# Running sums of a chunked down projection: kept in SBUF by VectorE, or in device memory by GpSimd's accumulating transfers

## The chip, the cores and the metric

The kernel runs on one core of a Trainium2 chip. The metric is the device time in microseconds (us). The kernel before takes 1972.66 us, the median of 3 runs (1972.44 to 1972.72). The engines are called PE (TensorE), ACT (ScalarE), DVE (VectorE), POOL (GpSimd) and SP (SyncE, which here issues transfers only).

## The reference: what is computed

One layer of a hybrid backbone on 128 context tokens and 256 latent tokens, with D_MODEL = 2048: an adaLN modulation, a mixing sub-layer (gated linear attention and a Fourier branch), and a feed-forward sub-layer. The change is in the second half of the last one:

```
h = rmsnorm(x, lw['norm_pre_ffn']) * (1.0 + sc2) + sh2
ff = (jax.nn.silu(h @ lw['w_ffn_gate']) * (h @ lw['w_ffn_up'])) @ lw['w_ffn_down']
x = x + ga2 * rmsnorm(ff, lw['norm_post_ffn'])
```

The hidden width is FFN_HIDDEN = 5632. All inputs and outputs are float32.

## The kernel before

All 384 tokens are worked on together, as three tiles of 128. The weights come from device memory once, in tiles of 128 x 1024 float32 (512 KB). Each tile is split into a rounded part `whi` (a cast by ACT, line 1393) and the rest `wlo` (a subtraction by DVE, line 1404), and each product is the sum of three matmul passes (whi with the high and the low part of the activations, wlo with the high part). `whi` and `wlo` have four buffers each, and the raw tiles have two (`raw`) or stand in eight resident places (`u...`). A tile of weights is therefore cast when the PE has finished the tile four steps earlier.

The hidden width is cut into NFC = 11 chunks of 512 columns. Chunk 0's hidden values are computed first, in another layout. Then the list `steps` is worked off, one weight tile per step. For each chunk c from 1 to 10 it holds steps A and B (four each), then C, E, D four times, then F, G, H, D four times. A, B, C, E, F, G and H compute the gate and up products of chunk c (seven products of half-size blocks instead of eight). Each D step multiplies the hidden values of chunk c - 1 by one tile of w_d: 18 matmuls of 128 x 512 (line 1492), and two D steps (kh = 0, 1) make one group n of 512 output columns in three PSUM tiles `pdn`, one for each token tile t. There are four groups n per chunk, so 12 tiles of 128 x 512. At the end stand eight D steps for chunk 10 alone, in the order n = 0, 2, 1, 3 (`d_order`).

The output sums lie in SBUF, in two tiles named `psums`; `unit(t, n)` is the place of one 128 x 512 tile. Products of chunks 0 to 9 are handled by `out` (lines 1566 to 1571), which frees the PSUM tiles. Small operations such as these are put in a list `pend`. `split_next` takes up to three of them between the cast and the subtraction of the next weight tile; whatever is left is taken before the next pair of D steps begins. Products of chunk 10 are added by `add_last` (line 1561), which also makes the sum of squares for the norm. Before chunk 10 begins (line 1578), `x1b`, the residual, is read from device memory in four transfers (line 1583). After the last product follow the norm factors, transposes on the PE (lines 1670 and 1672), the residual addition (DVE line 1706, or ACT line 1699 with POOL line 1700) and the output writes (line 1711).

Program order is kept on PE, ACT, DVE and POOL. The instructions of SP, which issues all loads, are put in order by a scheduler; each of them waits in a queue until its buffer is free. The loads of raw tiles are line 1363, those of the resident places line 1371, and those of the last modulation vector (`ada_last`, worked in between the steps) line 1430.

Of the kernel before, what the change touches and what calls it, by code (L numbers as in the profile page):

```python
# [11 lines left out]
F32 = mybir.dt.float32  # L12
# [3 lines left out]
ALU = mybir.AluOpType  # L16
# [4 lines left out]
P = 128  # L21
# [75 lines left out]
def tile_step(ctx: ExitStack, tc: tile.TileContext, a, o):  # L97
    nc = tc.nc
    PE, ACT, DVE, POOL, SP = nc.tensor, nc.scalar, nc.vector, nc.gpsimd, nc.sync
# [5 lines left out]
    dram = ctx.enter_context(tc.tile_pool(name="dram", bufs=1, space=DRAM))  # L105
# [138 lines left out]
    def step(side):  # L244
        if side is not None:
            next(side, None)
# [595 lines left out]
    with ExitStack() as s:  # L842
# [166 lines left out]
        for b, i in mix_order:  # L1009
# [9 lines left out]
            else:  # L1019
# [3 lines left out]
                p = psm.tile([P, T], F32, tag="mm", name="pmm")  # L1023
# [16 lines left out]
    with ExitStack() as s:  # L1040
# [94 lines left out]
        u = pd.tile([P, 2, 3], F32, name="u12", bufs=1)  # L1135
# [141 lines left out]
        def unit(t, n):  # L1277

            return psums[n // 2][:, 3 * (n % 2) + t, :]
# [10 lines left out]
        pend, now = [], []  # L1290

        def left_sums():

            raw = [psums[n // 3][:, 2 * (n % 3) : 2 * (n % 3) + 2, :].rearrange("p a (b c) -> p (a b) c", c=P) for n in range(4)]
            f = lambda x: x.bitcast(F32)
            h11, h12, h21, h22 = ([f(x) for x in Hx(t, k)] for t, k in ((1, 0), (1, 8), (2, 0), (2, 8)))
            r1, r2, r4, r3 = raw
            add, sub = DVE.tensor_add, DVE.tensor_sub

            def parts(dst, src):  # L1300
                return [lambda: ACT.copy(dst[0], src), lambda: sub(dst[1], src, f(dst[0]))]
# [22 lines left out]
        d_order = (0, 2, 1, 3)  # L1324
# [88 lines left out]
        def grab2(kept=2):  # L1413
            w = take()
            while now:
                now.pop(0)()
            load_more(kept)
            split_next()
            return w
# [52 lines left out]
        for u in range(HEAD):  # L1472
            kind, c, j = ffn_order[u]
            dst_of[kind](hp[u], c, j)
        n = 0
        for kind, c, j in ffn_order[HEAD:]:
            p = psm.tile([P, T], F32, tag="mm", name="pmm")
# [83 lines left out]
        def add_last(t, n, p, done):  # L1561

            DVE.tensor_add(unit(t, n), unit(t, n), p)
            ACT.activation(ep[0], unit(t, n), AF.Square, accum_out=ssq[:, t, done : done + 1])

        def out(u, p, c):
            if c == 0:
                ACT.copy(u, p)
            else:
                DVE.tensor_add(u, u, p)  # L1570
            d_live[0] -= 1

        rate[0] = 0.85
        ada = paced(ada_last(), rate)
        pd_tiles, hid_last, x1b, done = None, None, None, 0
        for kind, c, i in steps:
            last_c = c == NFC - 1 and kind == "D"
            if last_c and hid_last is not None and x1b is None:
                while pend:
                    pend.pop(0)()  # L1580
                x1b = actp.tile([P, KT, T], F32, tag="A_hi", name="x1b")
                for q in range(4):
                    SP.dma_start(x1b[:, 4 * q : 4 * q + 4, :], x1_d[:, 4 * q : 4 * q + 4, :])
                ACT.activation(tmp1, eps_t, AF.Sqrt)
            if kind == "D":
                w = grab2()
                n, kh = i // 2, i % 2
                if kh == 0:
                    while pend:
                        pend.pop(0)()  # L1590

                    pool, tag = (pss, "side") if done % 2 or (c, n) == (NFC - 2, 3) else (psm, "mm")
                    pd_tiles = [pool.tile([P, 512], F32, tag=tag, name="pdn") for _ in range(3)]
                    d_live[0] = 3
                h = hid_last if last_c else hid
                todo = [
                    (pd_tiles[t], [[x[:, 2 * kh + m, t * P : (t + 1) * P] for m in range(2)] for x in h], mov_d, kh == 0, kh == 1)
                    for t in range(3)
                ]
                products(w, todo, by_tile=last_c and kh == 1)  # L1600
                if kh == 1:
                    if not last_c:
                        for t in range(3):
                            pend.append(lambda u=unit(t, n), p=pd_tiles[t], c=c: out(u, p, c))
                    else:
                        if done < 3:
                            for t in range(3):
                                pend.append(lambda t=t, n=n, p=pd_tiles[t], d=done: add_last(t, n, p, d))
                        if done == 1:
                            pend.append(lambda: DVE.tensor_add(r3, ssq[:, :, 0], ssq[:, :, 1]))  # L1610
                        if done == 2:
                            pend.append(lambda: DVE.tensor_add(r3, r3, ssq[:, :, 2]))
                        done += 1
                if not last_c and i >= 4:
                    step(ada)
                if (c, i) == (NFC - 2, 6):

                    while pend:
                        pend.pop(0)()
                    hid_last = tuple(actp.tile([P, FC, T], F32R, tag=t, name="hidE") for t in ("C_hi", "C_lo"))  # L1620
                    for t in range(3):
                        turn_hid(hid_last, t, psm, "mm")
            else:
                if kind == "A" and i == 0:
                    banks(c)
                w = grab2()
                products(w, [(bank[c, n], two_of(stat, i), mov_gu, first and i == 0, i == 3 and last) for n, stat, first, last in of_kind[kind]])
                if i == 3:
                    evict(c, kind)
                if kind == "B" and c > 1 and i < 3:  # L1630

# [13 lines left out]
        n = d_order[-1]  # L1645
# [144 lines left out]
```

## Time and profile before

| What | Value |
|---|---|
| Median of 3 runs | 1972.66 us (1972.44 to 1972.72) |
| Profiled execution, first to last instruction | 1970.6 us |
| Median of the runs less that span | 2.1 us |
| Granted TensorE clock, mean | 0.999 |
| Bytes moved by transfers | 380.06 MB, mean 193 GB/s |
| Of these by SP's queue (q1) | 377.92 MB, 57.3% of 16 engines' span |
| GpSimd's own queue | not used |

The profile is of one execution. A row of a group gives the source line, the engine, the operation, output <- inputs, shapes and the number of instructions, then the busy time, the mean duration of one in ns, and the idle time of the engine just before them with what ended it. In a row of the order of time the first number is the start in us, the second the duration; an idle time before the instruction stands in brackets. Matmuls are pipelined: one of 128 x 512 is shown with 389 ns, and the next starts 227 ns after it (18 of them take 4.08 us).

### The profile page before, as it was taken

To read this page: it belongs to the slowest core of one execution; us is meant where nothing else is said; L and a number is where in the kernel's file an instruction comes from. 1 tells how busy PE (TensorE), PEld (TensorE's weight loads), DVE (VectorE), ACT (ScalarE), POOL (GpSimd) and SP (SyncE) were. 2 spreads that over 40 slices of the span, in tenths; PEclk is the share of its full clock that TensorE was granted. 3 is DMA by queue.
4 is the path that set the end of the run, shared out by engine and by line. 5 is a ranking of instruction groups with operands and counts; after the bars stand their busy time and mean duration, and the time that the engine had idled before them with its cause. 6 is when DMAs were issued, how large, how long until landed. Compare 5 with 4: busy or idle time off the path is not lost.

```text
span 1970.6 us, 27516 instructions
## 1 busy us (share of the span) xinstructions
PE 1949.7 (99%) x10576; PEld 1727.3 (88%) x10576; DVE 1629.0 (83%) x2075; ACT 908.9 (46%) x1281; POOL 32.2 (2%) x44
## 2 busy tenths in 40 slices
PE   8999999999999999999999999999999999999998
PEld 6779999999999999999988888888888888888886
DVE  5569788878767878877789998999899989887875
ACT  4233554544345655446454444354444444444444
POOL 0000000000000000004000000000000000000001
PEclk9999999999999999999999999999999999999999
DMA  9978677767755687555435444453536363626243
GB/s 389 369 258 271 219 254 238 234 217 247 232 182 180 195 296 233 203 171 180 142 133 183 145 148 156 160 182 123 190 131 201 104 204 109 205 75 192 74 160 130
DMA packets 189411, 380.06 MB, mean 193 GB/s; under 512 B 14172, under 2 KB 112668, under 8 KB 184928
## 3 DMA queue, kind: packets, MB, share of 16 engines
q1 hardware_dynamic: 189136, 377.92, 57.3%
q8 instruction: 83, 1.36, 0.3%
q14 instruction: 48, 0.39, 0.1%
q10 hardware_dynamic: 144, 0.39, 0.1%
HBM read 361.48 MB, written 16.78 MB: 192 GB/s over the span
## 4 chain that ended last, share of the span: by engine, by line
PE 93%; DVE 3%; ACT 2%; DMA 1%; issue 1%; SPq 0%; POOL 0%; DVEq 0%; ACTq 0%; POOLq 0%
PE pmm L252 33%; PE pgu L1492 30%; PE pdn L1492 18%; PE pv L392 3%; PE pgm L375 1%; DMA slab<-in_w_ada 1%; PE px L410 1%; PE pmm L1246 1%; PE ptr L1553 1%; PE pf L990 1%; DVE wlo L219 1%; ACT whi L218 1%; PE po L639 1%; DMA raw<-in_w_d 0%; PE pf L991 0%
## 5 line engine op out<-in xcount | busy, mean ns | idle before, releaser
L252 PE MATMUL pmm<-A_hi,whi 128*128 128x384 f32 x1200 | 404.2, 337 | 0.0
L252 PE MATMUL pmm<-A_hi,wlo 128*128 128x384 f32 x1200 | 401.3, 334 | 0.0
L252 PE MATMUL pmm<-A_lo,whi 128*128 128x384 f32 x1200 | 401.2, 334 | 0.0
L1393 ACT CAST whi<-u 128x1024 fp32r<-128x1024 f32 x200 | 210.6, 1053 | 286.8 <-DVE u L1377 86.2
L1393 ACT CAST whi<-raw 128x1024 fp32r<-128x1024 f32 x175 | 184.3, 1053 | 199.0 <-PE pgu L1492 60.4
L218 ACT CAST whi<-raw 128x1024 fp32r<-128x1024 f32 x181 | 189.9, 1051 | 176.6 <-DMA raw<-in_w_gate 62.4
L1404 DVE TENSOR_TENSOR wlo<-u,whi 128x1024 fp32r<-128x1024 f32 x200 | 243.8, 1219 | 33.0 <-ACT whi L1393 17.8
L219 DVE TENSOR_TENSOR wlo<-raw,whi 128x1024 fp32r<-128x1024 f32 x179 | 217.9, 1221 | 62.1 <-ACT whi L218 61.7
L1492 PE MATMUL pgu<-whi,A_hi 128*128 128x512 f32 x640 | 250.0, 391 | 0.0
L1492 PE MATMUL pgu<-whi,A_lo 128*128 128x512 f32 x640 | 249.3, 389 | 0.0
L1404 DVE TENSOR_TENSOR wlo<-raw,whi 128x1024 fp32r<-128x1024 f32 x175 | 213.2, 1218 | 34.8 <-ACT whi L1393 25.4
L252 PEld LDWEIGHTS pmm<-A_hi,whi 128*128 128x128 f32 x1200 | 225.3, 188 | 2.5 <-issue 1.4
L252 PEld LDWEIGHTS pmm<-A_lo,whi 128*128 128x128 f32 x1200 | 225.4, 188 | 0.2
L252 PEld LDWEIGHTS pmm<-A_hi,wlo 128*128 128x128 f32 x1200 | 225.3, 188 | 0.0
L566 DVE SCALAR_TENSOR_TENSOR adacc<-adaw,spad,adacc 128x1024 f32<-128x1024 f32 x180 | 222.7, 1279 | 0.6 <-DMA adaw<-in_w_ada 0.4
L1492 PE MATMUL pdn<-whi,hid_hi 128*128 128x512 f32 x480 | 186.9, 389 | 0.0
L1492 PE MATMUL pdn<-whi,hid_lo 128*128 128x512 f32 x480 | 186.8, 389 | 0.0
L1492 PE MATMUL pgu<-wlo,A_hi 128*128 128x512 f32 x640 | 184.2, 389 | 0.0
L1492 PEld LDWEIGHTS pgu<-whi,A_hi 128*128 128x128 f32 x640 | 120.1, 188 | 26.1 <-issue 0.8
L1492 PEld LDWEIGHTS pgu<-wlo,A_hi 128*128 128x128 f32 x640 | 120.1, 188 | 25.4
L1492 PEld LDWEIGHTS pgu<-whi,A_lo 128*128 128x128 f32 x640 | 120.2, 188 | 25.1
L1492 PE MATMUL pgu<-whi,S 128*128 128x512 f32 x480 | 131.1, 395 | 0.0
(367 smaller groups left out, 2768.2 us busy)
## 6 DMA issues: line engine op xcount, KB each, us to landing
adaw<-in_w_ada SPq DMA_DIRECT2D x96, 512.0 KB, 4.4
raw<-in_w_d SPq DMA_DIRECT2D x88, 512.0 KB, 3.7
slab<-in_w_ada SPq DMA_DIRECT2D x32, 1024.0 KB
raw<-in_w_gate SPq DMA_DIRECT2D x64, 512.0 KB, 4.6
raw<-in_w_g SPq DMA_DIRECT2D x48, 512.0 KB, 3.2
raw<-in_w_u SPq DMA_DIRECT2D x48, 512.0 KB, 3.4
raw<-in_w_in SPq DMA_DIRECT2D x44, 512.0 KB, 3.5
u<-in_w_u SPq DMA_DIRECT2D x40, 512.0 KB, 4.7
```

The source lines that it names most:

```text
L218: ACT.copy(hi, raw)
L219: sub = lambda: eng.tensor_sub(lo, raw, hi.bitcast(F32))
L252: PE.matmul(dst, w[wi][:, k * n + n0 : k * n + n0 + P], x[xi][:, k0 + k, :], start=first and k == 0 and j == 0, stop=last and k == kts - 1 ...
L375: PE.matmul(pgv[q : q + 32, :], spad[:, k, :], slab[k // (KT // 2)][:, k % (KT // 2), :], start=k < 4, stop=k >= KT - 4,)
L392: PE.matmul(pv[2 * t + g], hT[x_][:, kb, t * P : (t + 1) * P], w_[:, g * 512 : (g + 1) * 512], start=kb == 0 and j == 0, stop=kb == KT - 1 ...
L410: PE.matmul(px, w_[:, u * P : (u + 1) * P], hT[x_][:, kb, :], start=j == 0, stop=j == 2)
L566: DVE.scalar_tensor_tensor(acc[:, c, :], w, spad[:, k, c : c + 1], acc[:, c, :], op0=ALU.mult, op1=ALU.add,)
L639: PE.matmul(dst, w[wi], x[xi], start=first and j == 0, stop=last and j == 2)
L990: PE.matmul(pf[:, 0 : 2 * HT], w[0][:, c], x[k], start=k == 0, stop=False)
L1393: ACT.copy(hi, src)
L1404: DVE.tensor_sub(lo, src, hi.bitcast(F32))
L1492: PE.matmul(dst, stat[x_][m], mov(w[w_], m), start=first and w_ == m == x_ == 0, stop=last and w_ == m == 1,)
```

## The change

The function `out` no longer adds into SBUF. ACT copies each product tile, of chunk 0 and of all others, into a staging place; the six tiles of the groups n = 1 and n = 3 serve as two staging places of three tiles, used in turn. For chunk 0 SP writes the staged tile to a new tensor `sums_d` in device memory. For chunks 1 to 9 GpSimd issues a transfer that adds the staged tile to the tile in device memory. Before chunk 10 begins, SP reads all twelve sums back into `unit(t, n)`, in the order of `d_order`, and `add_last` goes on as before. Lines below 1563 are shifted by up to 13 in the changed kernel.

```
+        sums_d = dram.tile([3, 4, P, 512], F32, name="sums_d")
+        turn = [0]
+
+        def out(t, n, p, c):
+
+            u = unit(t, 1 + 2 * (turn[0] // 3 % 2))
+            turn[0] += 1
+            ACT.copy(u, p)
             if c == 0:
-                ACT.copy(u, p)
+                SP.dma_start(sums_d[t, n], u)
             else:
-                DVE.tensor_add(u, u, p)
+                POOL.dma_start(sums_d[t, n], u, accum_op=ALU.add)
             d_live[0] -= 1
+
+        def sums_back(n):
+            for t in range(3):
+                SP.dma_start(unit(t, n), sums_d[t, n])
...
                 while pend:
                     pend.pop(0)()
+                for n in d_order:
+                    sums_back(n)
                 x1b = actp.tile([P, KT, T], F32, tag="A_hi", name="x1b")
...
-                            pend.append(lambda u=unit(t, n), p=pd_tiles[t], c=c: out(u, p, c))
+                            pend.append(lambda t=t, n=n, p=pd_tiles[t], c=c: out(t, n, p, c))
```

The built order of the changed kernel has the same matmuls in the same order on the PE. DVE has 108 instructions fewer, ACT 108 more, POOL 108 transfers more (all between its last work of the layer before and the six additions of the tail), and SP 24 transfers more: 12 writes and 12 reads. The reads of n = 0 stand in SP's order after the fourth-last load of w_u, those of n = 2 and n = 1 among the loads of w_d that follow the last load of w_u, and those of n = 3 after the four loads of x1b and ahead of the last four loads of w_d.

More of the change, by code (lines that the diff above doesn't have):

```diff
@@ L1564, in add_last @@
             ACT.activation(ep[0], unit(t, n), AF.Square, accum_out=ssq[:, t, done : done + 1])
-        def out(u, p, c):
+        sums_d = dram.tile([3, 4, P, 512], F32, name="sums_d")
[4 more added lines that the diff above has]
+            ACT.copy(u, p)
             if c == 0:
-                ACT.copy(u, p)
+                SP.dma_start(sums_d[t, n], u)
             else:
-                DVE.tensor_add(u, u, p)
+                POOL.dma_start(sums_d[t, n], u, accum_op=ALU.add)
             d_live[0] -= 1
+        def sums_back(n):
+            for t in range(3):
+                SP.dma_start(unit(t, n), sums_d[t, n])
         rate[0] = 0.85
```

## Prediction

> **What bounds the kernel now.** I read the shares first, then the chain that ended last, then the busy time by stretch of the stage that is changed.
>
> ```profile
> span 1970.6 us, 27516 instructions
> ...
> PE 1949.7 (99%) x10576; PEld 1727.3 (88%) x10576; DVE 1629.0 (83%) x2075; ACT 908.9 (46%) x1281; POOL 32.2 (2%) x44
> ...
> PE 93%; DVE 3%; ACT 2%; DMA 1%; issue 1%; SPq 0%; POOL 0%; DVEq 0%; ACTq 0%; POOLq 0%
> ```
>
> TensorE is busy in 99% of the span and makes up 93% of the chain. VectorE, which the change relieves, is second with 83%. A share is an average, so the question is whether TensorE ever waits in the feed-forward stage. The busy time by stretch (columns: PE, PEld, DVE, ACT, POOL, granted clock, DMA share, GB/s) shows three chunks of that stage, the end of the last mixed chunk, the chunk of w_d alone and the tail:
>
> ```profile
> 995.90:1090.34 94.44, 94.44 (x424) 78.21 (x423) 83.74 (x88) 48.17 (x57) 0.00 (x0) 1.00 0.50 163
> ```
> ```profile
> 1090.34:1185.28 94.94, 94.94 (x439) 78.12 (x438) 85.89 (x95) 44.18 (x48) 0.00 (x0) 1.00 0.46 148
> 1185.28:1279.22 93.94, 93.94 (x422) 77.76 (x421) 85.66 (x97) 39.91 (x42) 0.00 (x0) 1.00 0.50 162
> ...
> 1845.86:1920.55 74.69, 74.69 (x338) 61.92 (x337) 59.50 (x63) 34.04 (x37) 0.00 (x0) 1.00 0.43 149
> 1920.55:1953.77 33.22, 33.09 (x145) 26.76 (x143) 17.02 (x25) 13.89 (x29) 0.00 (x0) 1.00 0.28 106
> 1953.77:1970.60 16.83, 8.25 (x65) 7.24 (x64) 9.92 (x31) 7.96 (x23) 5.87 (x6) 0.95 0.48 188
> ```
>
> In each stretch up to 1920.55 the PE column equals the length, at a clock of 1.00: TensorE does not wait at all while VectorE is at 91%. From 1920.55 to 1953.77 it lacks 0.13 us. A waiting weight load in that stage is listed once, with 0.6 us:
>
> ```profile
> PEld pdn L1492 <- DVE hidE L1555: 0.6, 1, 0.6
> ```
>
> So VectorE time that is taken out here has no stall behind it to shorten. A busy PE need not be a PE at its peak, but its pace here is set by its own matmuls.
>
> **The change part by part.** *Removed:* 108 VectorE adds.
>
> ```profile
> L1570 DVE TENSOR_TENSOR psums<-psums,pdn 128x512 f32<-128x512 f32 x108 | 67.6, 680 | 12.3 <-PE pdn L1492 12.3
> ```
>
> They are 67.6 us of busy VectorE, and by the stretches above worth 0 on the path.
>
> *Added on ScalarE:* 108 copies of the same tiles. The trace has the very operation, because the products of chunk 0 are copied today:
>
> ```profile
> L1568 ACT COPY psums<-pdn x12: 572/590/606, 1016.7 to 1070.5; 128x512 f32<-128x512 f32 x12
> ```
> ```profile
> 1015.70 1.05 ACT L1393 CAST whi<-raw 128x1024 fp32r<-128x1024 f32 x1 [3.32 <-DMA raw<-in_w_g]
> 1016.66 1.56 ACT L1568 COPY psums<-pdn 128x512 f32<-128x512 f32 x3
> ```
>
> Three take 1.56 us, so 36 groups are 36 x 1.56 = 56 us of ScalarE, spread over ten stretches in which it is busy about 45%. The first stretch above (995.90 to 1090.34) is the one with these twelve copies, at the same places in the step order, and TensorE is busy 94.44 of 94.44 us in it. So the copies, and the later casts queued behind them, cost 0. The spare that hides them can be read at one weight tile of w_g:
>
> ```profile
> 1851.77 0.37 SPq L1363 DMA_DIRECT2D raw<-in_w_g  x1
> ```
> ```profile
> 1855.51 1.06 ACT L1393 CAST whi<-raw 128x1024 fp32r<-128x1024 f32 x1 [2.12 <-PE pdn L1492]
> ```
> ```profile
> 1857.35 1.22 DVE L1404 TENSOR_TENSOR wlo<-raw,whi 128x1024 fp32r<-128x1024 f32 x1
> ```
> ```profile
> 1864.95 4.08 PE pgu L1492 x18
> ```
>
> The cast waits for the buffer of the tile four steps earlier (the w_d step before), so this tile belongs to the step that starts at 1864.95, and it is ready at 1857.35 + 1.22 = 1858.6. That is 6.4 us early. A delay under 6 us of a cast or a load is hidden here.
>
> *Added on the queues:* 12 plain writes by SyncE (chunk 0), 108 accumulating transfers by GpSimd, 12 reads by SyncE, 256 KB each. GpSimd's only row in the stage says that it sat idle for 1025.59 us before the tail,
>
> ```profile
> 1958.33 1.96 POOL L1700 TENSOR_TENSOR x1b<-x1b,ep 128x384 f32<-128x384 f32 x2 [1025.59 <-ACT ep L1699]
> ```
>
> so its instructions delay nothing but each other. The staging place is used again two groups later, about 2 x 94.4 / 4 = 47 us, so a copy would wait only for a transfer that takes longer than that. The trace has no accumulating transfer; the nearest rows are these (KB each, median us from issue to landing):
>
> ```profile
> w<-in_w_ada SPq DMA_DIRECT2D x64, 256.0 KB, 2.5
> gates_d<-gz SPq DMA_DIRECT2D x32, 192.0 KB, 3.8
> gate<-gates_d SPq DMA_DIRECT2D x32, 192.0 KB, 3.9
> ```
> ```profile
> raw<-in_w_d SPq DMA_DIRECT2D x88, 512.0 KB, 3.7
> ```
>
> Lower end: a plain 256 KB move, 2.5 us. Upper end: a read of the old value and a write one after the other, scaled to 256 KB, (3.8 + 3.9) x 4/3 = 10.3 us, and for the last of three behind each other two more moves of 2 x 256 KB at the 3.7 us of a 512 KB load of w_d (last row): 10.3 + 7.4 = 17.7. I take a load plus a write, 2.5 + 3.8 = 6.3 us, since the three of a group overlap and the load row is the one with the right size. The Trainium skill, "DMA: Bandwidth & Descriptors", section "Anatomy of one DMA — SWDGE (gpsimd) path", fits a GpSimd transfer with about 2.0 us plus bytes / 436e3; for 256 KB that makes an estimate of 2.6 us, by which the sum would be the same and its spare larger. No run so far shows such a transfer.
>
> Volume: 12 transfers of a chunk, each counted twice for the old value, are 12 x 0.262 x 2 = 6.3 MB. The second stretch moves 148 GB/s at a share of 0.46, so 322 GB/s when busy; 6.3 MB are 20 us, and the share goes from about 0.48 to 0.69. No queue saturates.
>
> *Moved: SyncE's queue at the end.* This is the tightest place. In the built order of the changed kernel the reads of n = 0 stand behind the load that is issued at 1869.39 today. Those of n = 2 and 1 stand between the loads of w_d issued at 1896.40 and 1913.69. Those of n = 3 stand behind all x1b loads and **ahead of the last four w_d loads**, which are issued from 1921.15 today:
>
> ```profile
> 1869.39 0.37 SPq L1363 DMA_DIRECT2D raw<-in_w_u  x1
> ```
> ```profile
> 1896.40 0.37 SPq L1363 DMA_DIRECT2D raw<-in_w_d  x1
> 1904.75 0.37 SPq L1363 DMA_DIRECT2D raw<-in_w_d  x1
> 1907.71 3.29 SPq L1363 DMA_DIRECT2D raw<-in_w_d  x2
> ```
> ```profile
> 1917.22 0.95 SPq L1583 DMA_DIRECT2D x1b<-x_d  x2
> 1921.15 11.37 SPq L1363 DMA_DIRECT2D raw<-in_w_d  x4
> ```
> ```profile
> 1899.44 1.88 DVE L1570 TENSOR_TENSOR psums<-psums,pdn 128x512 f32<-128x512 f32 x3 [1.27 <-PE pdn L1492]
> ```
>
> n = 2: the tiles are free at 1899.4, ScalarE has copied by about 1901.7, and at 6.3 us the last transfer lands at 1908.0. The load of 1904.75 waits only for the first one (1900.6 + 6.3 = 1906.9, 2.2 us late), the next pair for the last (0.3 us late). Both are under the 6 us of spare: 0.
>
> n = 3: its last product tile is done as the first hidE matmuls start, and today the cast behind the wait is this:
>
> ```profile
> 1920.55 3.31 PE L1492 MATMUL pdn<-whi,hidE 128*128 128x512 f32 x12
> ```
> ```profile
> 1918.65 1.55 ACT L1555 CAST hidE<-ptr 128x512 fp32r<-128x512 f32 x3
> ...
> 1921.63 1.03 ACT L1393 CAST whi<-raw 128x1024 fp32r<-128x1024 f32 x1
> 1926.90 1.05 ACT L1393 CAST whi<-raw 128x1024 fp32r<-128x1024 f32 x1 [4.24 <-DMA raw<-in_w_d]
> ```
>
> ScalarE goes on to the three copies at 1920.2 and ends them near 1922.0. The cast of 1921.63 slips about 2 us; its step comes at 1932.8, so 0. The last transfer lands at 1922.0 + 6.3 = 1928.3; three reads are issued in 3 x 0.35 = 1.05 us; the fifth w_d load goes out at 1929.4, 8.2 us later than today. With the 5.75 us that it takes today (1921.15 to 1926.90, beside the x1b traffic) it lands at 1935.1, and its cast ends at 1936.1. The steps are 18 matmuls or 4.08 us, so step five starts at 1920.6 + 4 x 4.08 = 1936.9. Spare 0.8 us: the stall is max(0, L - 7.1) for a transfer time L. At 6.3 it is 0, at 2.5 it is 0, at 17.7 it is 10.6 us. The loads behind it follow at the pace of two buffers and lose no more. The sums of n = 3 are wanted here, and are back near 1933; the tail is untouched:
>
> ```profile
> 1951.09 0.69 DVE L1563 TENSOR_TENSOR psums<-psums,pdn 128x512 f32<-128x512 f32 x1 [3.74 <-PE pdn L1492]
> ```
>
> **Sum.** Own time: span 1970.6, and 2.1 us around it to the median of 1972.66 (1972.44 to 1972.72). Removed 0, copies 0, traffic 0, n = 2 0, n = 3 0 to 10.6 with 0 taken. I add 0.6 us for a spare of only 0.8 us under new traffic (an estimate: the reads' 0.75 MB at 322 GB/s are 2.3 us, of which 2.3 - 0.8 = 1.5 would show if all fell on the load; I take less than half). Prediction **1973.3 us**.
>
> **The rivals.**
>
> *Slower 1: the last wait in SyncE's queue.* If a transfer needs 11 us or more after its copy, the four w_d loads come too late: at 12 us 4.9 us of stall, 1977.6; at 17.7 us 1983.3. It decides from 7.1 us, and is a measurable loss from 11. For it: nothing else lies between the reads and the loads. Against it: the rows of 2.5 to 3.9 us. 0.18.
>
> *Slower 2: weight loads slowed by the transfers in every chunk.* It needs more than the 6.4 us of spare. If three transfers held the engines 7.4 us, 36 x 1.0 = 36 us, 2009. Against it: the load of 1921.15 took 5.75 us beside x1b, about 2 us more than usual, and TensorE did not wait. The Trainium skill speaks for it, in "DMA: Bandwidth & Descriptors", section "Issuing engines are not separate DMA queues": transfers of all issuing engines run on the same 16 engines and interleave. 0.08.
>
> *Slower 3: the transfers don't keep up.* Three must be through in 94.4 / 4 = 23.6 us, 7.9 each. At 10 us each a group lacks 6.4 us, 36 groups 230 us, 2200. 0.03.
>
> *Faster.* A gain of over 0.2% needs 3.9 us of TensorE's waits in this stage, and 0.6 us are listed. It would have to come from matmuls that run faster beside a quieter VectorE:
>
> ```profile
> L1492 PE MATMUL pdn<-whi,hid_hi 128*128 128x512 f32 x480 | 186.9, 389 | 0.0
> ```
>
> The stage is ten stretches of some 430 matmuls (424, 439, 422 above); 1 ns less on each of 4300 is 4.3 us, 1968.4. Nothing in the trace points to it. 0.03.
>
> *The change does nothing:* the forecast, with chance 0.68; the VectorE time comes out idle.
>
> **How the numbers follow.** Within 0.2% (1968.7 to 1976.6, about what a measurement of this kernel can tell from no change): 0.68. Slower: 0.18 + 0.08 + 0.03 = 0.29. Faster 0.03. The range goes from 1971.8 (the median less the 0.6 us wait and a little) to 1983.5, the upper end of the unknown transfer time; what lies beyond is slower 2 and 3 and faster, 0.14.
>
> **What would show it.** Right: DVE about 68 us less, ACT about 56 us more, TensorE's column equal to the length in the stretches up to 1920, transfers under 7 us, and no wait of the PE on whi after 1936. Wrong: a wait of SyncE at the reads of n = 3 longer than 9 us with the casts of the fifth w_d tile after 1937; casts that wait for raw tiles all over the stage; copies that wait for a transfer out of their staging place; or, for the gain, matmuls shorter than 389 ns.

## The result, and the profile after

The changed kernel is slower: 1980.73 us, the median of 4 runs (1980.45 to 1982.1), against 1972.69 us (1972.44 to 1973.94, 4 runs) for the kernel before on the same chip. The ratio is 1.0042, 95% interval 1.0028 to 1.0057: 8.0 us. The profiled execution of the changed kernel has a span of 1979.1 us, 8.5 more than before.

The page of the changed kernel (shares, GpSimd's queue, shares of the chain):

```profile
PE 1950.5 (99%) x10576; PEld 1726.2 (87%) x10576; DVE 1569.2 (79%) x1967; ACT 955.5 (48%) x1389; POOL 127.6 (6%) x152
...
q0 software_dynamic: 15552, 28.32, 9.5%
...
PE 74%; issue 16%; DVE 3%; DMA 2%; POOL 2%; ACT 2%; SPq 0%; DVEq 0%; POOLq 0%; ACTq 0%
```

TensorE has the same work (1950.5 us against 1949.7) and VectorE 59.8 us less. No engine is busier in a way that makes 8.5 us; the loss must be idle time of TensorE. The busy time by stretch, with the stretches laid at the marks of the changed kernel, shows where it is (same columns as before):

```profile
995.90:1090.34 94.44, 94.44 (x424) 78.17 (x424) 83.73 (x88) 47.87 (x57) 0.00 (x0) 1.00 0.58 196
1090.34:1185.28 94.94, 94.94 (x440) 78.12 (x439) 79.49 (x83) 49.77 (x60) 10.74 (x12) 1.00 0.68 181
1185.28:1279.22 93.94, 93.94 (x422) 77.75 (x422) 78.58 (x84) 45.32 (x54) 10.58 (x12) 1.00 0.70 195
1845.71:1924.91 79.20, 76.19 (x341) 62.22 (x339) 54.49 (x54) 37.93 (x46) 7.93 (x9) 1.00 0.68 193
1924.91:1961.71 36.80, 33.48 (x145) 26.80 (x145) 16.80 (x28) 17.19 (x37) 2.65 (x3) 1.00 0.52 157
1961.71:1979.10 17.39, 8.25 (x64) 7.23 (x64) 8.52 (x26) 6.74 (x19) 5.87 (x6) 0.82 0.47 182
```

In the ordinary chunks the PE column is still the whole length, though the DMA share is 0.68 to 0.70. In the last mixed chunk TensorE lacks 79.20 - 76.19 = 3.01 us, and in the chunk of w_d alone 36.80 - 33.48 = 3.32. The last stretch is longer with the same 8.25 us of matmuls. Here are the same two stretches of the kernel before, between the same marks, and its tail; TensorE lacks nothing in the first and 1.75 us in the second, 1.62 of them at its end, where the norm factor is awaited in both kernels:

```profile
1845.26:1920.32 75.06, 75.06 (x341) 62.33 (x339) 59.87 (x63) 34.18 (x38) 0.00 (x0) 1.00 0.44 148
1920.32:1955.40 35.08, 33.33 (x147) 26.96 (x145) 18.66 (x31) 15.35 (x33) 0.00 (x0) 1.00 0.28 103
1955.40:1970.60 15.20, 8.24 (x64) 7.23 (x64) 8.51 (x26) 6.74 (x19) 5.87 (x6) 0.95 0.53 208
```

So the span's 8.5 us fall into pieces. The marks are five rows of each trace: the first product matmul of the stage (`pdn`), the transposes that end chunk 9's hidden values (line 1553), the first and the last row of the hidE weight loads, and ScalarE's issue of the last output write. Between the last hidE weight loads and that issue every profile has 12.98 to 13.01 us, so this piece is left out. The table has all profiled runs; the labels are those of the experiments below. The last column is the longest DRAIN of GpSimd at the end of the program.

| Profile | accumulating transfers | chunks ahead | last mixed chunk | hidE steps | last issue to end | drain |
|---|---|---|---|---|---|---|
| before | 0 | 842.17 | 75.06 | 32.61 | 4.68 | 1.43 |
| after | 108 | 842.52 | 79.20 | 34.32 | 6.87 | 8.12 |
| e1_reads_on_gpsimd | 108 | 843.78 | 79.60 | 34.00 | 4.94 | 2.45 |
| e2_no_reads | 108 | 843.51 | 77.14 | 32.87 | 6.79 | 8.12 |
| e3_one_gpsimd_transfer | 0 (1 plain) | 842.18 | 75.06 | 32.67 | 4.67 | 1.54 |
| e4_flush_first | 108 | 842.65 | 79.18 | 35.31 | 6.78 | 8.12 |
| e5_double_adds | 216 | 902.38 | 84.08 | 35.64 | 6.99 | 8.28 |
| e6_epilogue_first | 108 | 845.21 | 80.96 | 34.54 | 6.81 | 8.12 |
| e7_no_reads_no_last_adds | 96 | 843.05 | 75.06 | 32.75 | 5.77 | 7.13 |
| e8_three_late_adds | 3 | 842.18 | 75.06 | 32.69 | 4.88 | 1.71 |
| e9_48_adds | 48 | 843.21 | 75.17 | 32.93 | 4.94 | 5.38 |
| e10_24_adds | 24 | 842.17 | 75.44 | 32.93 | 4.92 | 3.42 |
| e11_reads_no_chunk9_adds | 96 | 844.15 | 75.58 | 32.92 | 5.86 | 7.14 |
| e12_only_chunk9_adds | 12 | 842.18 | 78.53 | 35.11 | 4.71 | 2.45 |

After against before: 0.35 + 4.14 + 1.71 + 2.19 = 8.4 us; the stage begins 0.1 later (1003.19 against 1003.09). What ended TensorE's idle time says which work was late. First the last mixed chunk and the hidE steps of the changed kernel (start, duration, idle time before in brackets):

```profile
1913.77 0.50 PE L1492 MATMUL pdn<-whi,hid_hi 128*128 128x512 f32 x1 [0.33 <-DVE ep L1542]
...
1918.52 0.66 PE L1553 MATMUL ptr<-ident,ep 128*128 128x128 f32 x4 [1.74 <-DVE ep L1543]
...
1919.84 0.66 PE L1553 MATMUL ptr<-ident,ep 128*128 128x128 f32 x4 [0.67 <-DVE ep L1546]
...
1924.91 1.20 PE L1492 MATMUL pdn<-whi,hidE 128*128 128x512 f32 x4 [0.27 <-DVE hidE L1555]
...
1943.50 2.97 PE L1492 MATMUL pdn<-whi,hidE 128*128 128x512 f32 x12 [1.14 <-DVE psums L1563]
```

Up to 1919.84 that is 2.74 us for VectorE's elementwise work on the last hidden values (`ep`), not for a weight tile. (The matmul column of this stretch is also 1.13 us longer than before, for the same 341 matmuls: the first one after a wait is shown longer, as in the first row with 0.50 us instead of 0.39.) VectorE in turn did nothing for a while just before it. These are VectorE's rows after, and then before, in the order of time:

```profile
1914.36 0.68 DVE L1543 TENSOR_TENSOR ep<-ep,pgu 128x512 f32<-128x512 f32 x1
1916.63 1.23 DVE L1404 TENSOR_TENSOR wlo<-raw,whi 128x1024 fp32r<-128x1024 f32 x1 [1.59 <-ACT whi L1393]
1917.78 0.69 DVE L1543 TENSOR_TENSOR ep<-ep,ep 128x512 f32<-128x512 f32 x1
...
1919.09 0.69 DVE L1546 TENSOR_TENSOR ep<-ep,ep 128x512 f32<-128x512 f32 x1
```
```profile
1912.44 1.22 DVE L1404 TENSOR_TENSOR wlo<-raw,whi 128x1024 fp32r<-128x1024 f32 x1
1913.58 0.68 DVE L1543 TENSOR_TENSOR ep<-ep,ep 128x512 f32<-128x512 f32 x1
...
1914.89 0.69 DVE L1546 TENSOR_TENSOR ep<-ep,ep 128x512 f32<-128x512 f32 x1
```

The subtraction for a w_d tile stands in VectorE's queue ahead of lines 1543 and 1546. Before, it starts at once; after, it waits 1.59 us for the cast, and the work behind it ends at 1919.78 instead of 1915.58. The cast waits for the load. ScalarE's casts and SyncE's queue of the changed kernel:

```profile
1910.81 1.05 ACT L1393 CAST whi<-raw 128x1024 fp32r<-128x1024 f32 x1 [3.93 <-DMA raw<-in_w_d]
1915.55 1.05 ACT L1393 CAST whi<-raw 128x1024 fp32r<-128x1024 f32 x1 [3.17 <-DMA raw<-in_w_d]
...
1940.45 1.05 ACT L1393 CAST whi<-raw 128x1024 fp32r<-128x1024 f32 x1 [11.43 <-DMA raw<-in_w_d]
```
```profile
1905.69 0.42 SPq L1363 DMA_DIRECT2D raw<-in_w_d  x1
1907.47 2.09 SPq L1582 DMA_DIRECT2D psums<-sums_d  x3
1909.66 0.38 SPq L1363 DMA_DIRECT2D raw<-in_w_d  x1
...
1933.07 3.05 SPq L1582 DMA_DIRECT2D psums<-sums_d  x3
1936.21 9.87 SPq L1363 DMA_DIRECT2D raw<-in_w_d  x4
```

And the casts of the same two tiles in the kernel before:

```profile
1908.29 1.05 ACT L1393 CAST whi<-raw 128x1024 fp32r<-128x1024 f32 x1 [1.87 <-DMA raw<-in_w_d]
1911.23 1.05 ACT L1393 CAST whi<-raw 128x1024 fp32r<-128x1024 f32 x1 [1.35 <-PE pgu L1492]
```

The second of them, the first tile of chunk 10, is 4.3 us later (3.9 if one allows for the start of the chunk, 1845.71 against 1845.26), and the idle time in its brackets has passed from TensorE to a transfer. Of the 2.5 us of the first, 0.9 are a later issue (1905.69 against 1904.75) and 1.6 a slower transfer: 5.1 us from issue to cast against 3.5. The load for the second is issued 1.95 us later (1909.66 against 1907.71), behind the reads, and takes 5.9 us from issue to cast. The issue table shows the slower transfers in general (KB each, median us to landing; w_d took 3.7 before):

```profile
raw<-in_w_d SPq DMA_DIRECT2D x87, 512.0 KB, 5.7
sums_d<-psums POOLq DMA_DIRECT2D x108, 256.0 KB, 6.9
...
psums<-sums_d SPq DMA_DIRECT2D x12, 256.0 KB, 5.7
```

The 2.2 us at the end are GpSimd's. At the end of the program it executes an instruction DRAIN. Its instructions of this kind on the program's last line, after and before (duration in ns: shortest, median, longest; first and last start):

```profile
L1793 POOLq DRAIN  x3: 40/102/8115, 1970.2 to 1978.8; - x3
```
```profile
L1780 POOLq DRAIN  x3: 34/78/1434, 1963.8 to 1970.3; - x3
```

After, the long drain runs from 1970.2 to 1978.3, and the program ends 0.8 us later. The last output write, issued at 1972.23, would have let it end at 1976.9, if it took the 4.7 us that it took before.

### The profile page after: what moved, and what is told of

Its sections match the earlier page's. It is cut to its first block, busy times and chain, and to the rows that moved or that the text cites. A ratio compares the mean times of both kernels' runs of the same rounds, so it can differ in the third digit from the quotient of the medians.

```text
span 1979.1 us, 27870 instructions
## 1 busy us (share of the span) xinstructions
PE 1950.5 (99%) x10576; PEld 1726.2 (87%) x10576; DVE 1569.2 (79%) x1967; ACT 955.5 (48%) x1389; POOL 127.6 (6%) x152
## 3 DMA queue, kind: packets, MB, share of 16 engines
q1 hardware_dynamic: 192592, 384.21, 57.5%
q0 software_dynamic: 15552, 28.32, 9.5%
## 4 chain that ended last, share of the span: by engine, by line
PE 74%; issue 16%; DVE 3%; DMA 2%; POOL 2%; ACT 2%; SPq 0%; DVEq 0%; POOLq 0%; ACTq 0%
PE pmm L252 33%; PE pgu L1492 20%; PE pdn L1492 11%; PE pv L392 3%; POOL sums_d L1577 2%; PE pgm L375 1%; DMA slab<-in_w_ada 1%; PE px L410 1%; PE pmm L1246 1%; DVE wlo L219 1%; ACT whi L218 1%; PE po L639 1%; DMA sums_d<-psums 0%; PE pf L990 0%; PE ptr L1553 0%
## 5 line engine op out<-in xcount | busy, mean ns | idle before, releaser
L1393 ACT CAST whi<-raw 128x1024 fp32r<-128x1024 f32 x175 | 184.3, 1053 | 246.0 <-DMA raw<-in_w_d 63.8
L1577 POOL DMA_DIRECT2D sums_d<-psums x108 | 95.4, 1214 | 900.3 <-ACT psums L1573 900.3
```

Source lines behind the costliest of these rows:

```text
L1393: ACT.copy(hi, src)
L1577: POOL.dma_start(sums_d[t, n], u, accum_op=ALU.add)
```

## The experiments

Each run is compared with the kernel before, timed beside it. The kernel before had 1972.8 us beside e1 to e4, 1973.04 beside e5 to e8, 1972.7 beside e9 to e11 and 1973.31 beside e12.

**e1_reads_on_gpsimd.** The changed kernel with the reads in GpSimd's queue, each group behind its own additions; SyncE's queue is free of them.

```
             for t in range(3):
-                SP.dma_start(unit(t, n), sums_d[t, n])
+                POOL.dma_start(unit(t, n), sums_d[t, n])
...
-                for n in d_order:
-                    sums_back(n)
...
+                        if c == NFC - 2:
+                            for m in {0: (), 1: (0,), 2: (2, 1), 3: (3,)}[n]:
+                                pend.append(lambda m=m: sums_back(m))
```

> The twelve reads of the sums are issued by GpSimd instead of SyncE, each group once its accumulation is done (n=0 after the copies of n=1, n=2 and n=1 after those of n=2, n=3 after its own); SyncE's loads stand in the order of the kernel before. The bytes moved are those of the change. Queue theory: the change loses about 6 us in the last 60 us of TensorE's work because w_d loads stand behind reads that wait for accumulating transfers in SyncE's queue; then these 6 us go, and about 1974.9 us is left (2.2 us of a longer end and 0.4 us stay). Traffic rival: the loads are late because reads and accumulations share the transfer engines with them; then the loss stays within 1 us, 1980.

Measured: 1981.59 us (1977.98 to 1983.06, 5 runs), ratio 1.0039 (1.0026 to 1.0053). The last mixed chunk still takes 79.60 us and the hidE steps 34.00. So ahead of hidE the order of SyncE's queue does not make the loss: with the wait for the additions gone from that queue, the loads of w_d are late all the same. The hidE steps are long here for another reason. The granted clock was 0.50 from 1928.25 to 1931.66, just after TensorE had waited 2.35 us for the first hidE matmul; there matmuls start up to 0.43 us apart instead of 0.23, and the first of the eight steps takes 6.12 us instead of 4.50. The later steps lose nothing. The end is 4.94 us, almost as before, and the drain 2.45.

**e2_no_reads.** No reads at all; GpSimd clears the places of n = 0 and n = 2 in SBUF instead. The output lacks the sums of chunks 0 to 8 and most of chunk 9.

```
-                SP.dma_start(unit(t, n), sums_d[t, n])
+                POOL.memset(unit(t, n), 0.0)
...
-                for n in d_order:
-                    sums_back(n)
...
+                        if (c, n) == (NFC - 2, 1):
+                            pend += [lambda: sums_back(0), lambda: sums_back(2)]
```

> The reads of the sums are left out: the places of n=0 and n=2 are zeroed by GpSimd and those of n=1 and n=3 keep the last staged tiles, so the sum over chunks 0 to 8 and most of chunk 9 is missing from the output. Everything else is as in the change. Queue theory: the same as with the reads on GpSimd's queue, about 1974.9 us. Traffic rival: better than that run by what 3.1 MB of reads cost the loads; if the whole 6 us are due to the reads' traffic, 1975 here and 1980 there.

Measured: 1977.83 us (1975.85 to 1980.86, 8 runs), ratio 1.0026 (1.0015 to 1.0036). The last mixed chunk keeps 2.08 us of its 4.14, and the hidE steps 0.26 of 1.71. Without the reads half of the loss ahead of hidE goes, and most of that behind it. The chain of e2 has the load that took 3.44 us before:

```profile
1905.07 6.61 DMA raw<-in_w_d
```

No read stands ahead of it, and it takes 6.6 us beside the additions of the group n = 2.

**e3_one_gpsimd_transfer.** The kernel before, with one plain transfer by GpSimd from SBUF to a spare tensor, early in the stage.

```
+        spare_d = dram.tile([P, 512], F32, name="spare_d")
...
+                        if (c, n) == (0, 0):
+                            pend.append(lambda: POOL.dma_start(spare_d, unit(0, 0)))
```

> The kernel before, with one plain 256 KB write added, issued by GpSimd near 1020 us into a scratch tensor. Theory of a fixed price: any transfer that GpSimd has issued makes its drain at the end of the program about 8.1 us long instead of 1.4, and the last instruction 2.2 us later relative to the last output write: 1974.9 us, drain 8 us. Rival: the drain grows with the number of transfers or with how late the last one was; then one early transfer leaves 1.4 us of drain and 1972.7.

Measured: 1972.87 us (1972.41 to 1973.71, 10 runs), ratio 1.0 (0.999 to 1.0009). One transfer in GpSimd's queue costs nothing by itself. It took 2.44 us from issue to landing, and the drain is 1.54 us.

**e4_flush_first.** The changed kernel, with the waiting small operations taken ahead of the step (9, 6), so that the last copies and additions would go earlier.

```
+                if (c, i) == (NFC - 2, 6):
+                    while pend:
+                        pend.pop(0)()
                 w = grab2()
```

> The change, with the pending epilogue operations of chunk 10's hidden values (VectorE lines 1542 to 1546, and their ScalarE ones) put ahead of the cast and the subtraction of the next w_d tile, at the step that begins group 3 of chunk 9. Theory: the stall of 2.4 us at the transposes comes from VectorE's in-order queue, where these operations stand behind the subtraction of a late w_d tile; then 2 to 3 us go, 1978. Rival: TensorE waits for the late w_d tile itself; then the stall only moves to the matmuls and the time stays at 1980.7.

Measured: 1983.72 us (1981.12 to 1985.66, 4 runs), ratio 1.0054 (1.0039 to 1.0069). The edit left VectorE's order as it was, so the run does not test what it was made for. It reads as the change once more: 79.18 in the last mixed chunk, and 35.31 in the hidE steps, where the changed kernel has 34.32.

**e5_double_adds.** Every write and every addition is made twice, the second time into a second tensor.

```
+        more_d = dram.tile([3, 4, P, 512], F32, name="more_d")
...
                 SP.dma_start(sums_d[t, n], u)
+                SP.dma_start(more_d[t, n], u)
             else:
                 POOL.dma_start(sums_d[t, n], u, accum_op=ALU.add)
+                POOL.dma_start(more_d[t, n], u, accum_op=ALU.add)
```

> The change with every write and every accumulating transfer issued twice, the second into a tensor that nobody reads. Theory that the spare of the ordinary chunks hides the transfers: from the first w_d product to the last transposes of chunk 10, 842.4 us before and 842.7 with the change, grows to at most 844. Rival, that the spare is nearly used up: six transfers a group hold the loads by more than their 6 us and this stretch grows by tens of us. Theory of the long drain as a matter of the number of transfers: 216 instead of 108 give a drain of about twice 8.1 us; as a fixed price 8.1.

Measured: 2043.42 us (2040.87 to 2047.35, 4 runs), ratio 1.0353 (1.0336 to 1.037). Now the chunks ahead take 60.2 us more. Their busy time by stretch, and what TensorE waits for ahead of 1905 us (total, times, longest):

```profile
1090.34:1197.14 106.80, 100.86 (x441) 81.40 (x440) 83.02 (x88) 49.97 (x61) 21.43 (x24) 0.95 0.79 195
1197.14:1296.00 98.86, 96.58 (x431) 79.03 (x431) 79.82 (x85) 45.44 (x55) 21.27 (x24) 1.00 0.84 216
```
```profile
PEld pgu L1492 <- ACT whi L1393: 25.7, 9, 4.4
PE pgu L1492 <- ACT whi L1393: 21.9, 9, 4.0
PEld pgu L1492 <- DVE wlo L1404: 16.9, 21, 3.2
```

TensorE now waits for casts and subtractions of weight tiles all over the stage, at a DMA share of 0.79 to 0.84. The spare of the ordinary chunks, which hides the additions once, does not hide them twice. Waiting is not all of the 60.2 us: in the chunks ahead TensorE is idle for 35.0 us and its matmuls are busy 867.3 us instead of 842.2, at a mean granted clock of 0.98 (0.95 in the first row above; 0.50 from 1158.1 to 1164.9).

**e6_epilogue_first.** The changed kernel, with the elementwise work on the last hidden values put ahead of the late tile's subtraction on VectorE.

```
-                w = grab2()
+                late = (kind, c, i) == ("H", NFC - 1, 3)
+                w = take() if late else grab2()
...
+                if late:
+                    while pend:
+                        pend.pop(0)()
+                    load_more(2)
+                    split_next()
```

> The change, with the cast and subtraction of the first w_d tile of chunk 10 moved behind the last epilogue operations of the hidden values (VectorE lines 1543 and 1546), which the edit before did not do. In the built order one more w_d load then also stands ahead of the reads of n=3. Theory: TensorE's 2.4 us at the transposes come from VectorE's in-order queue behind the late tile, so from the last transposes of chunk 10's gate products to the first hidE matmul it takes 76.5 to 77 us instead of 79.2 (75.0 before); and with the fifth w_d load ahead of the waiting reads, the hidE matmuls take 32.4 us instead of 34.1. Together 1976.5. Rival: the tile itself is late for TensorE; then the first of the two stays at 79.

Measured: 1983.06 us (1982.66 to 1985.58, 4 runs), ratio 1.0054 (1.0039 to 1.0069): no gain, and the last mixed chunk takes 80.96 us. The waits of the transposes for lines 1543 and 1546 are gone, but TensorE waits once, and longer, at the first hidE matmul:

```profile
1929.46 5.41 PE L1492 MATMUL pdn<-whi,hidE 128*128 128x512 f32 x12 [4.26 <-DVE hidE L1555]
```

This wait goes back to ScalarE: its copies of the transposed values, from 1928.11 on, stand behind a cast that waited 5.28 us for its load. So the order of the work on VectorE and ScalarE decides where the late tiles are felt: in the changed kernel and in e6 alike it is by the work behind their casts and subtractions. For its own matmuls the first w_d tile of chunk 10 was not late even in the changed kernel: it was ready at 1917.86, and its step began at 1924.91. In e6 the granted clock was 0.50 from 1927.79 to 1934.62, around the end of this wait, so the first hidE step takes 6.64 us instead of 4.50; step five, whose load here stands ahead of the waiting reads, starts without a wait.

**e7_no_reads_no_last_adds.** As e2, and without the additions of chunk 9.

```
-            else:
+            elif c < NFC - 2:
                 POOL.dma_start(sums_d[t, n], u, accum_op=ALU.add)
```

> As without reads, and chunk 9's accumulating transfers are left out too (the output lacks the sums). Traffic theory: the 2.1 us that were left before the first hidE matmul without the reads come from the three transfers of n=2 that slow the w_d load of group 3; then the stretch from the transposes to the first hidE matmul is back at 75.0 us. Rival: they come from the copies on ScalarE; then it stays at 77.1. The last transfer of GpSimd is now about 90 us earlier: if the long drain depends on the lateness of the last accumulating transfer it is back at 1.4 us, if on their presence it stays at 8.1.

Measured: 1975.93 us (1974.5 to 1977.81, 10 runs), ratio 1.0015 (1.0005 to 1.0024). The last mixed chunk is 75.06 us again, to the digit, and the hidE steps 32.75. What is left is 0.88 in the chunks ahead and 1.09 at the end, where the drain takes 7.13 us; the stage also began 1.5 us later in this execution, in which the granted clock was 0.50 for 6.8 us near 698 us (before: for 3.4).

**e8_three_late_adds.** The kernel before with three plain writes by SyncE and three accumulating transfers by GpSimd at the end of chunk 9, into a spare tensor.

```
+        spare_d = dram.tile([3, P, 512], F32, name="spare_d")
...
+                        if (c, n) == (1, 0):
+                            pend += [lambda t=t: SP.dma_start(spare_d[t], unit(t, 0)) for t in range(3)]
+                        if (c, n) == (NFC - 2, 3):
+                            pend += [lambda t=t: POOL.dma_start(spare_d[t], unit(t, 3), accum_op=ALU.add) for t in range(3)]
```

> The kernel before, with three writes by SyncE at chunk 1 and three accumulating transfers by GpSimd at the end of chunk 9 into a scratch tensor. If a late accumulating transfer makes the drain long: 8.1 us and 2.2 us more at the end, 1975. If it is their number: 1.5 us and 1972.8.

Measured: 1973.02 us (1972.79 to 1975.48, 10 runs), ratio 1.0002 (0.9993 to 1.0011). Three additions late in the stage, with nothing waiting for them, cost nothing, and the drain is 1.71 us.

**e9_48_adds and e10_24_adds.** As e7, with additions for chunks 1 to 4 and for chunks 1 and 2 only, to see what the drain counts.

```
-            elif c < NFC - 2:
+            elif c < 5:
```
```
-            elif c < NFC - 2:
+            elif c < 3:
```

> The kernel without reads, with accumulating transfers for chunks 1 to 4 only (48; the products of chunks 5 to 10 are left out of the sums, and the sums start from zero in SBUF). With 96 transfers GpSimd's last drain took 7.13 us, with 3 it took 1.71, with none 1.43. Theory: the drain settles something for each transfer since the start, 0.06 us each ((7.13 - 1.43) / 96), so 48 give 1.43 + 48 x 0.06 = 4.3 us, which is hidden before the last output has landed, and the time is within 0.1% of the kernel before. Rival: the drain goes by what was issued lately, so that 48 transfers that ended some 500 us ahead give 1.4 us. Second rival: any long list of transfers costs the same, 7 us.

> As the run with 48, with accumulating transfers for chunks 1 and 2 only (24; the products of chunks 3 to 10 are left out of the sums). Theory of 0.06 us for each: a drain of 1.43 + 24 x 0.06 = 2.9 us. Rivals: 1.4 us, or 7 us. The time is within 0.1% of the kernel before in every case but the last, which gives 1 us more.

Measured: e9 1975.77 us (1972.87 to 1977.39, 10 runs), ratio 1.0012 (1.0002 to 1.0021); e10 1973.31 us (1972.21 to 1974.78, 10 runs), ratio 1.0003 (0.9994 to 1.0012). The drains are these, e10 first:

```profile
L1793 POOLq DRAIN  x3: 40/93/3421, 1964.2 to 1971.0; - x3
```
```profile
L1793 POOLq DRAIN  x3: 40/102/5379, 1966.9 to 1973.7; - x3
```

(3.42 - 1.43) / 24 and (5.38 - 1.43) / 48 are both 0.08 us for each transfer, above the 0.06 expected: the drain does grow with what was issued since the start, however long ago, and both rivals fall. But 96 transfers then lack 2.2 us (1.43 + 96 x 0.082 = 9.3, measured 7.13). From 96 to 108 the drain grows by 0.08 us each once more (8.12), and 216 have no more than 8.28. The time of e9 is 0.12% above the kernel before, a little more than expected, with 1.04 us of it in the chunks ahead; the stage also began 1.58 us later, with the clock as in e7.

**e11_reads_no_chunk9_adds.** The changed kernel with the reads, without the additions of chunk 9. The edit is that of e7, in the changed kernel; the scheduler puts the first reads earlier.

> The changed kernel with all twelve reads, without the twelve accumulating transfers of chunk 9 (its products are left out of the sums). The run without reads lost 2.1 us ahead of the first hidE matmul, the changed kernel 4.15, the run without both nothing. Theory: traffic of the last chunk adds up, so the reads alone make the w_d tiles late by about 2 us there, 1 us more in the hidE steps, and 1.1 us at the end by GpSimd's drain: about 1977. Rival: the wait of the reads for the transfers is what delays the loads queued behind them; without those transfers nothing waits, the stretch ahead of hidE is 75.0 us as before, and the time is 1975.5 to 1976, like the run without both.

Measured: 1976.26 us (1974.66 to 1978.68, 10 runs), ratio 1.0018 (1.0008 to 1.0027). The last mixed chunk takes 75.58 us, 0.52 more than before, and the hidE steps 0.31. The reads alone cost 0.5 ahead of hidE, the additions alone 2.1 (e2), both 4.1: they do not add up, since only what exceeds the spare shows. The rival expected here, that the wait of the reads for the additions matters, is nearer to the number. For the stretch ahead of hidE e1 has shown that the place of that wait does not matter; for step five of the hidE steps it does, as the next section shows.

**e12_only_chunk9_adds.** The same kernel with the additions of chunk 9 alone.

```
-            else:
+            elif c == NFC - 2:
                 POOL.dma_start(sums_d[t, n], u, accum_op=ALU.add)
```

> The changed kernel with all twelve reads and with the twelve accumulating transfers of chunk 9 alone; those of chunks 1 to 8 are left out, so the sums lack these products. The order on every engine and in SyncE's queue is that of the changed kernel. Theory: the loss ahead of and in the hidE steps is made there, by the transfers that run beside the last loads of w_d. So the stretch to the first hidE weight load stays near 79.2 us and the hidE steps near 34.3, as in the changed kernel; the chunks ahead take 842.2 us as in the kernel before, GpSimd's last drain is 1.43 + 12 x 0.082 = 2.4 us, and the last output ends the program: about 5.9 us above the kernel before, 1978.6. Rival: the 96 earlier transfers leave something behind that slows the late ones or GpSimd; then the two stretches shrink towards 75.1 and 32.6, and the time is near 1973.

Measured: 1979.52 us (1978.71 to 1980.12, 7 runs), ratio 1.0031 (1.0019 to 1.0042). The chunks ahead are as before (842.18), the last mixed chunk takes 78.53 us and the hidE steps 35.11, the drain 2.45. So twelve of the 108 additions, with the twelve reads, make 3.47 + 2.50 = 6.0 of the 8.0 us. The waits of TensorE and its weight loads from 1840 us on name the same lines as in the changed kernel:

```profile
PEld pdn L1492 <- ACT whi L1393: 2.3, 1, 2.3
...
PE pdn L1492 <- DVE psums L1563: 1.9, 1, 1.9
...
PE pdn L1492 <- DVE ep L1542: 0.9, 1, 0.9
PE ptr L1553 <- DVE ep L1543: 0.7, 1, 0.7
PE ptr L1553 <- DVE ep L1546: 0.7, 1, 0.7
```

## Why the prediction was right in the chunks and wrong at their end

The time lies in the range (1971.8 to 1983.5), but most of the chance was on no change, and the likeliest case was not the one that came. That the range holds it is luck: its upper end was for slow transfers at n = 3, while 4.1 us of the loss came at n = 2 and 2.2 us in the tail, both put at 0.

*Removed adds, 0:* right. VectorE has 59.8 us less (forecast 68) and TensorE gains nothing in any stretch. *Copies, 0:* right in the ordinary chunks, where the PE column is full. ScalarE has 46.6 us more, not 56. But the copies are not quite free: in seven of the ten profiles that have them with up to 108 additions (e1, e2, e4, e6, e7, e9 and e11), TensorE waits once for a copy, between 1490 and 1494 us, for 0.16 to 1.03 us. In e2 and e9 that copy stands on ScalarE behind a cast that had waited 2.4 and 2.3 us for its w_g tile. I had looked at casts behind copies, and not at copies behind late casts.

*Traffic, 0:* right in the changed kernel's ordinary chunks up to 0.35 us over ten chunks. The share forecast (0.69) was met (0.68 to 0.70), though not by counted bytes: the profile counts an addition's bytes once (28.32 MB for 108), at 9.5% of 16 engines' span, which is 151 GB/s while busy, where SyncE's queue has 338 (384.21 MB at 57.5%). That the read of the old value takes this time is not shown. And the margin is thin. The profiles with 96 or 108 additions lose 0.35 to 3.04 us in the chunks ahead, the one with 48 loses 1.04, those with 24 or fewer, or none, 0.0; e5 with twice the additions loses 60 us. So "Slower 2" becomes true somewhere between one and two additions per tile. The Trainium skill, "DMA: Bandwidth & Descriptors", section "Issuing engines are not separate DMA queues", says that transfers of all issuing engines share the same 16 engines; e1 and e2 agree with it: a load that stands behind no read took 6.6 us instead of 3.4, and moving the reads to another queue left 79.6 us.

*Transfer time, 6.3 us:* near. The median of 108 transfers is 6.9 us, the range 3.8 to 10.6. The Trainium skill's fit in "Anatomy of one DMA — SWDGE (gpsimd) path", same page, gives an estimate of 2.6 us. The one plain transfer of e3, with 2.44 us, is near it; not one of the 108 accumulating ones was that short, so for these, beside loads, the measurement decides.

*n = 2, "under the 6 us of spare: 0":* this is the step that failed. I had read the spare at one w_g tile in the middle of a chunk, 6.4 us, and used it for a w_d tile at the end of the stage. At the issue the lateness was of the size worked out, though not load by load: the load forecast 2.2 us late went out 0.9 late, the next one, forecast 0.3 late, went out 1.95 late. What I left out is that both also took longer (1.6 us for the first, and 5.9 us for the second where the median before was 3.7), and what stands behind the tile. VectorE's subtraction of that tile is ahead of lines 1543 and 1546, which the transposes of the last hidden values need. In the kernel before these lines end at 1915.58, and the twelve transposes go in one run:

```profile
1915.11 1.47 PE L1553 MATMUL ptr<-ident,ep 128*128 128x128 f32 x12
```

The last four of them need line 1546 about 0.9 us into this run, so they had some 0.4 us of spare. A tile 3.9 us late in its chunk has to show: 2.74 us are idle time at lines 1542 to 1546, and the whole stretch grew by 4.14. That another order moves the wait and does not end it is shown by e6; that the late transfers are the cause is shown by e7 (both taken out: 75.06) and e12 (of the additions only these kept, with the reads: 78.53).

*n = 3, a stall of max(0, L - 7.1):* a wait came at the step named, but not in the way worked out. The last addition took 8.78 us, and 8.78 - 7.1 = 1.7 is the loss of the hidE steps (1.71) to the digit. That is chance:

```profile
1926.97 8.78 DMA sums_d<-psums
```

The reads then took 0.46 us instead of 1.05 (the fifth load went out at 1936.21), and the load 4.24 us to its cast instead of 5.75. So this cast ended at 1941.50, 0.7 us before step five was due (1938.12 + 4.08 = 1942.20), and by the formula's own terms there would be no stall. TensorE waited for VectorE's addition of the first hidE product (line 1563), which frees a PSUM tile that step five writes, and which stands behind the subtraction of the fifth tile. VectorE after, and the same addition before:

```profile
1941.53 1.23 DVE L1404 TENSOR_TENSOR wlo<-raw,whi 128x1024 fp32r<-128x1024 f32 x1 [11.25 <-ACT whi L1393]
1942.67 1.88 DVE L1563 TENSOR_TENSOR psums<-psums,pdn 128x512 f32<-128x512 f32 x3
```
```profile
1929.12 1.88 DVE L1563 TENSOR_TENSOR psums<-psums,pdn 128x512 f32<-128x512 f32 x3
```

Step five began at 1943.50, 1.30 us late; most of the rest of the 1.71 is a wait of the first step for line 1555 (0.54 us). The queue that the prediction named is the cause here. Step five began late in the four profiles whose fifth load stands behind reads that wait for additions (1.30 us after, 2.28 in e4, 2.58 in e5, 2.06 in e12), and without a wait in all the others, e1, e2, e6 and e11 among them. So "Slower 1" came, with a chance of 0.18, at a shorter transfer than its 11 us and through work that the prediction did not look at; it is the smaller part of the loss.

*"The tail is untouched":* wrong by 2.2 us. I had looked for work of the kernel and not for what the program does at its end. That the drain takes 7.1 to 8.3 us with 96 transfers or more and 1.4 to 5.4 with 48 or fewer is measured; that it sets the end there follows from the times (it ends 0.8 us ahead of the program in the changed kernel, and e1, with a drain of 2.45, has 4.94 us at the end). Why it grows unevenly above 48, and why e1 with 120 transfers has the drain of e12 with 12, was not settled.

What would have shown it: the wait of the casts for raw w_d tiles was named as a sign of failure, and it is there (63.8 us in total against 23.6), but "after 1937" was the wrong place; the first that hurt are at 1910.81 (0.33 us, at line 1542) and 1915.55.

## What to carry to other kernels

Measure the spare at the very tile that becomes late, and follow what stands behind it on each engine that works in order: a weight tile with microseconds to spare for its own matmuls may have none for the work queued behind its subtraction, the elementwise work at n = 2 and the freeing of a PSUM tile at n = 3. Transfers that cost little in the middle of a stage (0.35 to 3.04 us over ten chunks), where the next weights are far ahead, cost more at its end, where loads, residual reads and the read-back of the results meet: 12 of the 108 additions made, with the twelve reads, three quarters of the loss. And work that is taken off an engine which nobody waits for buys nothing (59.8 us of VectorE here), while its replacement uses up a spare that somebody may need.

## What the runs showed of the hardware

An accumulating transfer of 256 KB issued by GpSimd took 3.8 to 10.6 us from issue to landing (median 6.9), and the 108 issues held GpSimd for 95.4 us, 0.88 us each, against 0.34 us of SyncE for a read of the same tile. Beside one such transfer for each product tile, the 512 KB loads of w_d took 5.7 us in place of 3.7.

After TensorE had waited 2.35 us (e1) and 4.26 us (e6) the granted clock was 0.50 for 3.4 and 6.8 us. No length of wait that decides it comes out of the runs: after 2.12 us (e4, at 1943.78) the clock stayed at 1.00, while in e5 it was 0.50 from 1120.5 to 1123.9, after a wait of 1.81 us.

GpSimd's drain at the end of the program keeps a cost for each transfer that it issued, 0.08 us each for 12, 24 and 48, though the last of the 48 was issued 515 us and the last of the 24 704 us ahead of the drain. It reached 8.1 us with 108 and then ended the program.
